# Another order of work and another set of load sizes for a sum of reciprocals

## The chip, the core and the metric

The kernel runs on one core of a Trainium2 chip. Five engines work side by side, each with its own queue of instructions that it runs in order: TensorE (PE in the profile) for matrix products, VectorE (DVE), ScalarE (ACT) and GpSimd (POOL) for elementwise work, and SyncE (SP), which here only issues transfers. Transfers from device memory (HBM) are carried out by 16 DMA engines. The metric is the time of one execution on the device, in microseconds (us); lower is better.

## What is computed

The input holds 32 x 512 = 16384 vectors of 1024 positive numbers in float32, 67.1 MB. The output is the sum of the reciprocals of each vector.

```python
x = np.abs(np.random.randn(32, 512, 1024)).astype(np.float32) + 1e-6

def reference(x):
    return np.sum(1.0 / x, axis=-1).astype(np.float32)
```

## The kernel before

**Tiling.** The 16384 vectors are laid over 128 partitions, 128 vectors on each. A "row" of the kernel is one vector on each partition: 128 partitions x 1024 numbers, 512 KB. There are 128 rows, 0 to 127. The last two, 126 and 127, are cut into halves of 512 columns. The halves have the numbers 126 to 129: first the left halves of both rows, then the right halves. So the list below counts 130 pieces.

**The arithmetic.** A row is halved, into x0 and x1 of 512 columns each, and 1/x0 + 1/x1 is taken as (x0 + x1) / (x0 x1). With S = 2^17 as a scale, ACT computes exp(-ln(S x0 x1)), which is the reciprocal of the product. Two ways lead from there to the sum:

- With an S step, PE adds the halves by two products with the identity matrix into one bank of PSUM (its accumulator memory, 8 banks). DVE then multiplies the 512 reciprocals by the 512 sums and accumulates.
- Without an S step, ACT writes its reciprocals into a PSUM bank, and DVE multiplies all 1024 inputs of the row by them (each reciprocal used twice) and accumulates. This leaves PE out and costs DVE more.

**The buffers.** `ring` holds 40 rows of input, and row q stands at place q % 40. A load of row q therefore waits until row q - 40 has been read for the last time. `prod` holds 22 slots of products, `ps` the 8 PSUM banks, `sums` the 128 results of each partition.

**The order.** Nothing is scheduled by a planner at build time. The order is the list `PLAN`, written out in the source, and the loop at its end issues each token in turn, so the order of the tokens of one engine is the order of that engine's queue. The number after the letter is the row (for D the number of rows), `+n` means n rows in one instruction, `@b` a bank or, for L, a slot:

- `D` (line 185, SP): load the next rows in one transfer. A load also waits, in this build, for the completion of the load eight before it, since eight completion counters are used in turn.
- `P` (line 197, POOL): the product x0 x1 into a slot. `C` with `V` (lines 207 and 218): the same product by PE and DVE, where PE first copies x1 into a bank. `W` (line 218): the same by DVE alone.
- `L` (line 240, ACT): Ln of the slot, with scale S. `E` (line 249, ACT): Exp of its negative, into the slot, or with `@b` into a bank.
- `S` (line 230, PE): the sum of the halves into a bank.
- `R` (line 265, DVE): the multiplication and the accumulation; it frees the bank, the slot and the place in the ring.

`place()` tells where a piece lies in its row. `rows()` names the parts of rows that a step touches, from which `note()` works out which waits are already implied by others. Everything is in one pass; the result is stored by one transfer at the end (line 282).

Two short stretches of the list of before show its style: pairs in the middle, single rows at the end.

```python
L26+2@4 C35@3 E26+2 S27@1 P30+2 V35 L28+2@8 R26 S30@2 R27 E28+2@6
L123@6 R122 L124@7 W125 S125@1 E123@7 E124@6 R123 P126
```

Of the kernel before, what the change touches and what calls it, by code (L numbers as in the profile page):

```python
# [11 lines left out]
def kernel(  # L12
# [9 lines left out]
    H = D // 2  # L22
    F = 128
    R = 40
    NP = 22
    LAST = F - 2  # L26
    S = float(2**17)


# [3 lines left out]

    PLAN = """
        D2 D10 D14 D14 P0+2 C3@3 S2@0 V3 P2 L0+2@0 C11@3 S3@1 E0+2@6 P4+2 V11 L2+2@2 R0 S6@2
        E2+2 R1 P6+2 L4+2@4 R2 R3 E4+2@6 S7@0 P8+2 L6+2@8 R4 S10@1 E6+2 R5 P10 L8+2@10 R6 R7
        S11@2 E8+2@6 L10+2@6 R8 E10+2 R9 D11 R10 R11 P12+2 C19@3 S14@0 V19 P14+2 L12+2@12  # L40
        S15@1 E12+2@6 S18@2 R12 P16+2 L14+2@16 R13 E14+2 R14 P18 L16+2@18 R15 S19@0 E16+2@6
        P20+2 L18+2@14 R16 S22@1 E18+2 R17 D9 P22+2 L20+2@20 R18 R19 E20+2@6 S23@2 P24+2
        L22+2@0 R20 E22+2 R21 L24+2@2 R22 R23 E24+2@6 P26 C27@3 R24 S26@0 P28+2 V27 R25 D7
        L26+2@4 C35@3 E26+2 S27@1 P30+2 V35 L28+2@8 R26 S30@2 R27 E28+2@6 P32+2 L30+2@10 R28
        S31@0 E30+2 R29 P34 L32+2@12 S34@1 R30 R31 E32+2@6 P36+2 S35@0 L34+2@6 R32 E34+2 R33
        D7 P38+2 S38@2 L36+2@16 R34 R35 E36+2@6 S39@1 P40+2 L38+2@18 R36 C43@3 E38+2 R37 D6
        S42@0 P42 L40+2@14 V43 R38 E40+2@6 P44+2 R39 S43@2 L42+2@20 R40 E42+2 S46@1 R41 D3
        P46+2 L44+2@0 R42 R43 E44+2@6 S47@0 P48+2 L46+2@2 R44 S50@2 E46+2 R45 P50 L48+2@4
        R46 C51@3 R47 E48+2@6 S51@1 P52+2 V51 R48 D6 L50+2@8 C59@3 E50+2 R49 P54+2 S54@0
        L52+2@10 V59 R50 E52+2@6 R51 S55@2 P56+2 L54+2@12 R52 E54+2 S58@1 R53 D5 P58  # L50
        L56+2@16 R54 R55 E56+2@6 S59@0 P60+2 L58+2@6 R56 S62@2 E58+2 R57 D4 P62+2 L60+2@14
        R58 R59 E60+2@6 S63@1 P64+2 L62+2@18 R60 S66@0 E62+2 R61 D4 P66 L64+2@20 R62 C67@3
        R63 E64+2@6 P68+2 S67@2 V67 R64 L66+2@0 S70@1 R65 D4 E66+2 P70+2 L68+2@2 R66 R67
        S71@0 E68+2@6 P72+2 L70+2@4 R68 D3 E70+2 R69 D2 C75@3 P74 L72+2@10 S74@2 R70 V75
        P76+2 E72+2@6 R71 S75@1 L74+2@8 R72 D2 E74+2 R73 D2 P80 S78@0 L76+2@12 R74 P81
        L80@16 R75 S79@2 E76+2@6 P78+2 L81@17 R76 D2 S81@1 E80@5 E81 R80 L78+2@6 W82 E78+2
        R81 R77 D1 D1 D1 D1 D1 P88 C85@6 S85@1 R78 P83 L88@18 V85 E88@7 R79 P84 S84@0
        L82+2@14 R88 E82+2@5 P86+2 L84+2@19 R82 D1 E84+2 R83 D1 D1 D1 C90@7 P91 L86+2@0
        S91@2 R85 P93 V90 E86+2@5 R84 P92 S90@1 L90+2@2 R87 L93@21 W89 L92@10 R86 D1 D1 D1
        D1 E93@7 P94 S97@0 E92@6 R93 E90+2 P97 S94@3 L89@11 R92 E89@7 P95 L97@8 R91 S95@4  # L60
        E97 R90 L94+2@4 W96 R97 P101 C99@6 L96@9 R89 E94+2 S100@0 P98 V99 E96@5 L101@12 R95
        P100 S99@1 L98@13 R96 E101@7 L99+2@16 R101 E98@6 P104 C103@5 R94 E99+2 S105@2 R98
        P102 L104@18 V103 E104@7 W105 L102+2@6 R100 P107+2 C106@6 L105@14 R104 E102+2@4
        S108@0 V106 E105 R102 L106+3@19 P109 S107@3 R103 P110 E106+3 R105 S106@4 R99 P111+2
        L109+2@0 R107 S112@1 R108 E109+2@6 R106 L111+2@10 P114 R109 S111@0 E111+2 R110 P113
        L114@15 R111 C115@7 P116 L113@2 R112 E114@6 V115 E113@5 S117@0 P117 R114 L116@3
        L115@8 P118 E116@7 R113 S118@1 E115@6 P119 L117+2@12 R116 E117+2 R115 P120 S120@2
        L119@9 R117 P121 L120@4 S121@3 R118 E119@7 E120 R119 P122 L121@5 S122@0 E121 R120
        P123 L122@18 R121 E122 W124 L123@6 R122 L124@7 W125 S125@1 E123@7 E124@6 R123 P126
        L125@14 P127 L126@16 S127@0 R124 E125 P128 L127@17 S128@2 E126@7 P129 R125 E127  # L70
        S129@3 L128@19 R126 L129@20 E128 R127 E129 R128 R129
    """.split()

    Ln = mybir.ActivationFunctionType.Ln
# [37 lines left out]
    def place(r):  # L112
        if r < LAST:
            return r, 0, H
        part, q = divmod(r - LAST, F - LAST)
        return LAST + q, part * H, H // 2

    def xs(r, h):
        q, at, w = place(r)
        return ring[:, q % R, at + h * w : at + (h + 1) * w]  # L120
# [43 lines left out]
    def rows(r, n, h=None):  # L164
        spaces = []
        for q, at, w in (place(i) for i in range(r, r + n)):
            end = at + 2 * w
            if h is not None:
                at, end = at + h * w, at + (h + 1) * w
            spaces += [("row", q % R, i) for i in range(at, end, H // 2)]  # L170
        return spaces

    def slots(r, n):
# [2 lines left out]
    with tc.manual_schedule():  # L176
        for op, r, n, b in ops:
            p = pslot.get(r)
            if op == "D":
                n, r = r, loaded  # L180
                while n:
                    q, at, w = place(r)
                    a = q % R
                    m = min(n, R - a, LAST - r) if r < LAST else 1
                    inst = nc.sync.dma_start(  # L185
                        out=ring[:, a : a + m, at : at + 2 * w],
                        in_=x_v[:, q : q + m, at : at + 2 * w],
                    )
                    note("SP", inst, writes=rows(r, m))
                    r, n = r + m, n - m  # L190
                loaded = r
            elif op == "P":
                while n:
                    q, at, w = place(r)
                    a, p = q % R, pslot[r]
                    m = min(n, R - a)
                    inst = nc.gpsimd.tensor_tensor(  # L197
                        out=prod[:, p : p + m, :w],
                        in0=ring[:, a : a + m, at : at + w],
                        in1=ring[:, a : a + m, at + w : at + 2 * w],  # L200
                        op=mult,
                    )
                    note("POOL", inst, rows(r, m), slots(r, m))
                    r, n = r + m, n - m
            elif op == "C":
# [6 lines left out]
                    stop=True,  # L212
                )
                note("PE", inst, rows(r, 1, 1), [("bank", b)])
            elif op in "WV":
                w = place(r)[2]
# [38 lines left out]
            elif op == "R":  # L255
                q, at, w = place(r)
                other = ps[:, bank[r], :w]
                if r in halves:
                    row = prod[:, p, :w]
                else:  # L260
                    row = ring[:, q % R, at : at + 2 * w]
                    row = row.rearrange("p (h e) -> p h e", h=2)
# [50 lines left out]
```

## Time and profile before

| | us |
|---|---|
| six runs, median (lowest to highest) | 168.38 (168.25 to 172.23) |
| the profiled execution | 168.25 |
| its span, first to last instruction | 166.4 |
| busy: PE, ACT | 132.5 each |
| busy: DVE, POOL | 128.4, 128.2 |
| share of the DMA engines' time in the loads | 95.1% |

The span is 1.85 us shorter than the time of its own execution. In the profile a row of slices has 40 digits, one for each fortieth of the span (4.16 us), in tenths of full use. "Landing" of a load means that all 16 DMA engines have reported their part. A wait names the last thing that released it. Of PE the list shows each 32-bit product as two matrix instructions, which is why an S step, with two products, makes four, and a C step two.

### The profile page before, as it was taken

Reading aid. Unit: us, or ns where it says so; the run is one execution under the profiler, and the core shown is the slowest. Engines: PE = TensorE matmul, PEld = TensorE weight load, DVE = VectorE, ACT = ScalarE, POOL = GpSimd, SP = SyncE. Lnnn points to the kernel's source line nnn. Section 1 sums busy time; section 2 is a strip of 40 time slices with the busy share of each in tenths; the row PEclk is TensorE's granted clock in tenths of the full one; section 3 lists DMA queues with packets and bytes.
Section 4 is the critical chain, followed back from the end, with each engine's and each line's share of the span. In section 5 each row is a group of like instructions: output and inputs, shape, how many; then the busy total and the mean of one; then the engine's idle time right before and its main releaser. Section 6 shows DMA issues by size and latency. Waiting matters only on the chain.

```text
span 166.4 us, 1340 instructions
## 1 busy us (share of the span) xinstructions
PE 132.5 (80%) x292; PEld 55.5 (33%) x292; DVE 128.4 (77%) x282; ACT 132.5 (80%) x157; POOL 128.2 (77%) x81
## 2 busy tenths in 40 slices
PE   0000799769956999999999999989599979989882
PEld 0000343234312444444433433334234324423351
DVE  0000149855787699799998898989999999999993
ACT  3040067919994899999799999997999998999992
POOL 1500795069995999999999999949977869999860
PEclk9999999969996999999999999999999999999999
DMA  5999999999998989999999999999999999999930
GB/s 195 530 394 394 441 441 441 441 441 441 441 441 381 487 379 424 429 423 438 434 441 441 410 419 458 411 422 430 417 429 433 418 414 425 411 408 410 400 113 18
DMA packets 4904, 67.26 MB, mean 404 GB/s; under 512 B 544, under 2 KB 672, under 8 KB 2336
## 3 DMA queue, kind: packets, MB, share of 16 engines
q1 hardware_dynamic: 4896, 67.18, 95.1%
q8 instruction: 2, 0.03, 0.1%
q14 instruction: 6, 0.05, 0.1%
HBM read 67.11 MB, written 0.07 MB: 404 GB/s over the span
## 4 chain that ended last, share of the span: by engine, by line
DMA 55%; PE 18%; POOL 9%; ACT 8%; DVE 6%; issue 2%; SPq 1%; POOLq 0%; DVEq 0%
DMA ring<-in_x_dram 55%; PE ps L230 15%; POOL prod L197 9%; ACT prod L240 4%; DVE ring L265 3%; PE ps L207 3%; ACT ps L249 3%; DVE prod L265 2%; ACT prod L249 2%; DVE prod L218 1%; SPq L185 1%; DVE sums L265 0%; POOLq L197 0%; DVEq L308 0%
## 5 line engine op out<-in xcount | busy, mean ns | idle before, releaser
L197 POOL TENSOR_TENSOR prod<-ring 128x1024 f32<-128x1024 f32 (+2 forms) x75 | 127.5, 1736 | 33.3 <-DMA ring<-in_x_dram 27.6
L230 PE MATMUL ps<-ring,ident 128*128 128x512 f32 (+1 forms) x260 | 116.4, 595 | 3.9 <-DVE sums L265 3.4
L240 ACT ACTIVATE prod<-prod 128x1024 f32<-128x1024 f32 (+2 forms) x78 | 68.6, 892 | 25.9 <-DVE prod L218 14.2
L265 DVE CUSTOM_DVE_ANT_1 ring<-ring,ps 128x1024 f32<-128x1024 f32 (+1 forms) x65 | 76.4, 1209 | 7.7 <-ACT ps L249 7.5
L230 PEld LDWEIGHTS ps<-ring,ident 128*128 128x128 f32 x260 | 49.5, 195 | 70.9 <-issue 53.0
L265 DVE CUSTOM_DVE_ANT_0 prod<-prod,ps 128x512 f32<-128x512 f32 (+1 forms) x63 | 41.0, 679 | 0.6 <-PE ps L230 0.4
L207 PE MATMUL ps<-ring,ident 128*128 128x512 f32 x32 | 19.9, 709 | 26.8 <-DMA ring<-in_x_dram 26.4
L249 ACT ACTIVATE ps<-prod 128x1024 f32<-128x1024 f32 (+2 forms) x41 | 34.1, 838 | 3.3 <-DVE sums L265 2.5
L249 ACT ACTIVATE prod<-prod 128x1024 f32<-128x1024 f32 (+3 forms) x37 | 34.4, 932 | 0.9
L218 DVE TENSOR_TENSOR prod<-ring,ps 128x512 f32<-128x512 f32 x16 | 11.0, 685 | 27.2 <-PE ps L207 27.2
L207 PEld LDWEIGHTS ps<-ring,ident 128*128 128x128 f32 x32 | 5.9, 212 | 36.4 <-issue 20.8
L265 DVE DVE_READ_ACCUMULATOR2_ANT sums<- 128x1 f32 x130 | 10.7, 83 | 0.0
L218 DVE TENSOR_TENSOR prod<-ring 128x512 f32<-128x512 f32 x6 | 4.1, 688 | 0.1
L83 ACT ACT_TABLE_LOAD x1 | 1.3, 1283 | 0.7 <-PEq L297 0.7
L265 DVE CUSTOM_DVE_ANT_0 prod<-prod,ps,sums 128x256 f32<-128x256 f32 x2 | 0.9, 476 | 0.0
masks.py:197 POOL MEMSET ident<- 128x128 f32 x1 | 0.2, 205 | 0.3 <-POOLq L297 0.3
masks.py:199 POOL TENSOR_SCALAR_AFFINE_SELECT ident<-ident 128x128 f32<-128x128 f32 x1 | 0.3, 294 | 0.1
L297 POOL MEMSET const-float32-0.0<- 128x1 f32 x1 | 0.1, 99 | 0.2 <-issue 0.2
L297 POOL MEMSET const-bfloat16-1.0<- 128x1 bf16 x1 | 0.1, 102 | 0.0
L297 POOL MEMSET const-uint8-127<- 128x1 uint8 x1 | 0.1, 102 | 0.0
L297 POOL MEMSET const-float32-1.0<- 128x1 f32 x1 | 0.1, 99 | 0.0
## 6 DMA issues: line engine op xcount, KB each, us to landing
ring<-in_x_dram SPq DMA_DIRECT2D x2, 7168.0 KB, 41.2
ring<-in_x_dram SPq DMA_DIRECT2D x2, 3584.0 KB, 29.2
ring<-in_x_dram SPq DMA_DIRECT2D x2, 3072.0 KB, 31.7
ring<-in_x_dram SPq DMA_DIRECT2D x3, 2048.0 KB, 33.7
ring<-in_x_dram SPq DMA_DIRECT2D x1, 5632.0 KB, 31.7
ring<-in_x_dram SPq DMA_DIRECT2D x5, 1024.0 KB, 32.0
ring<-in_x_dram SPq DMA_DIRECT2D x1, 5120.0 KB, 16.5
ring<-in_x_dram SPq DMA_DIRECT2D x1, 4608.0 KB, 30.8
```

What stands on the lines that cost most here:

```text
L83: nc.scalar.add_instruction(mybir.InstLoadActFuncSet(name=nc.get_next_instruction_name(), act_func_set_id=act_sets.index("natural_log_exp_ ...
L185: inst = nc.sync.dma_start(out=ring[:, a : a + m, at : at + 2 * w], in_=x_v[:, q : q + m, at : at + 2 * w],)
L197: inst = nc.gpsimd.tensor_tensor(out=prod[:, p : p + m, :w], in0=ring[:, a : a + m, at : at + w], in1=ring[:, a : a + m, at + w : at + 2 * w],
L207: inst = nc.tensor.matmul(ps[:, b, : place(r)[2]], lhsT=ident, rhs=xs(r, 1), start=True, stop=True,)
L218: inst = nc.vector.tensor_tensor(out=prod[:, p, :w], in0=xs(r, 0), in1=in1, op=mult)
L230: inst = nc.tensor.matmul(ps[:, b, : place(r)[2]], lhsT=ident, rhs=xs(r, h), start=h == 0, stop=h == 1,)
L240: inst = nc.scalar.activation(out=pg, in_=pg, func=Ln, scale=S)
L249: inst = nc.scalar.activation(out=rc, in_=pg, func=Exp, scale=-1.0)
L265: inst = nc.vector.tensor_tensor_reduce(out=row, in0=row, in1=other, scale=S, scalar=total if q in summed else 0.0, op0=mult, op1=add, acc ...
L297: nc = _bacc.Bacc("TRN2", target_bir_lowering=False, num_devices=1)
```

## The change

The list is replaced by another that loads 2, 10, 16, 12, 12, 10, 9, 3, 6, 7, 6, 5, 4, 2, 3, 3 rows, then five times 2, then six single rows and the four half rows: 31 loads in place of 33. The first 40 rows, which fill the ring, come as 2, 10, 16 and 12 rows instead of 2, 10, 14 and 14. The steps of rows 12 to 79 keep their kind with a few moves (row 27 gets its product by C and V earlier in the list, some slots and banks are others). From row 80 on rows are taken in another order, other rows get S steps, and other rows are grouped. In all, one row more has an S step (66 instead of 65, of 130), V and W stay at 16 and 6, ACT has one triple more and two pairs fewer of Ln (48) as well as of Exp (48), and six rather than nine single rows are loaded at the end.

The half rows are now written as a table, `PARTS`, with the same four halves in the same order, and `rows()` names parts of 128 columns instead of 256.

```diff
-    LAST = F - 2
+    PARTS = [(126, 0, 512), (127, 0, 512), (126, 512, 512), (127, 512, 512)]
+    LAST = PARTS[0][0]
     S = float(2**17)
     PLAN = """
-        D2 D10 D14 D14 P0+2 C3@3 S2@0 V3 P2 L0+2@0 C11@3 S3@1 E0+2@6 P4+2 V11 L2+2@2 R0 S6@2
+        D2 D10 D16 D12 P0+2 C3@3 S2@0 V3 P2 L0+2@0 C11@3 S3@1 E0+2@6 P4+2 V11 L2+2@2 R0 S6@2
...
-        S11@2 E8+2@6 L10+2@6 R8 E10+2 R9 D11 R10 R11 P12+2 C19@3 S14@0 V19 P14+2 L12+2@12
-        S15@1 E12+2@6 S18@2 R12 P16+2 L14+2@16 R13 E14+2 R14 P18 L16+2@18 R15 S19@0 E16+2@6
+        S11@2 E8+2@6 L10+2@6 R8 E10+2 R9 D12 R10 R11 P12+2 C19@3 S14@0 V19 P14+2 L12+2@12
+        C27@3 S15@1 E12+2@6 V27 R12 P16+2 L14+2@16 S18@2 R13 E14+2 R14 P18 L16+2@20 R15
...
-        P76+2 E72+2@6 R71 S75@1 L74+2@8 R72 D2 E74+2 R73 D2 P80 S78@0 L76+2@12 R74 P81
-        L80@16 R75 S79@2 E76+2@6 P78+2 L81@17 R76 D2 S81@1 E80@5 E81 R80 L78+2@6 W82 E78+2
-        R81 R77 D1 D1 D1 D1 D1 P88 C85@6 S85@1 R78 P83 L88@18 V85 E88@7 R79 P84 S84@0
+        P76+2 R71 S75@1 L74+2@4 R72 E74+2 S78@2 R73 D2 D2 P78+2 L76+2@12 R74 R75 E76+2@6
+        S79@0 L78+2@16 R76 P80 C83@5 E78+2 R77 D2 D2 P81 S84@1 L80@20 V83 E80@7 P84 R78
+        L81@21 S83@3 R80 D1 L83@10 P85 E81@6 R79 E83 S82@2 W82 L84@11 W86 E84 L82@2 R83
+        L85+2@14 R81 D1 D1 D1 D1 P90+2 S87@0 E82 R84 E85+2@6 R82 C92@5 R85 D1 P87+3 L90+2@0
+        S88@1 V92 E90+2@3 R86 D1 D1 D1 D1 S89@2 L92@3 R91 E92@6 L87+3@6 P97 C96@7 R90 S96@4
...
+        L94+2@4 R96 S101@0 V98 E93@6 P99 E94+2@4 R93 S103@1 P101+2 L99+2@12 R94 L98@20 R95
+        E99+2@6 S102@2 P103 E98@4 R100 S104@3 P105 L101+3@14 R98 P106 R99 E101+3 P104
...
+        S113@0 R108 P112 L113@6 E110+2 R109 P115 S115@3 E113 R110 L112@7 P114 L115@8 R113
+        E112@7 R111 S117@0 E115 P116 R112 L114@18 E114@6 W117 L116@19 R114 L117@9 P118
+        C119@7 E116@5 R115 S119@1 E117 V119 P120 L118@4 R117 L119@5 R116 E118@7 P121 S121@2
+        E119 R118 L120@12 P122 L121@13 S122@0 E120@6 R119 E121 W123 L122@20 R120 S123@1
+        L123@14 P124 E122 R121 E123 W125 S124@3 L124@15 R122 P126 L125@16 R123 E124 P127
+        S126@0 E125@7 R124 P128 L127@11 S128@1 R125 L126@10 P129 E127@6 E126 S129@2 L129@1
+        R127 L128@0 R126 E129 E128 R129 R128
     """.split()
...
-        part, q = divmod(r - LAST, F - LAST)
-        return LAST + q, part * H, H // 2
+        q, at, length = PARTS[r - LAST]
+        return q, at, length // 2
...
-            spaces += [("row", q % R, i) for i in range(at, end, H // 2)]
+            spaces += [("row", q % R, i) for i in range(at, end, H // 4)]
```

More of the change, by code (lines that the diff above doesn't have):

```diff
@@ L25 @@
     NP = 22
-    LAST = F - 2
+    PARTS = [(126, 0, 512), (127, 0, 512), (126, 512, 512), (127, 512, 512)]
+    LAST = PARTS[0][0]
     S = float(2**17)
     PLAN = """
-        D2 D10 D14 D14 P0+2 C3@3 S2@0 V3 P2 L0+2@0 C11@3 S3@1 E0+2@6 P4+2 V11 L2+2@2 R0 S6@2
+        D2 D10 D16 D12 P0+2 C3@3 S2@0 V3 P2 L0+2@0 C11@3 S3@1 E0+2@6 P4+2 V11 L2+2@2 R0 S6@2
         E2+2 R1 P6+2 L4+2@4 R2 R3 E4+2@6 S7@0 P8+2 L6+2@8 R4 S10@1 E6+2 R5 P10 L8+2@10 R6 R7
-        S11@2 E8+2@6 L10+2@6 R8 E10+2 R9 D11 R10 R11 P12+2 C19@3 S14@0 V19 P14+2 L12+2@12
-        S15@1 E12+2@6 S18@2 R12 P16+2 L14+2@16 R13 E14+2 R14 P18 L16+2@18 R15 S19@0 E16+2@6
[L42 to L54, printed above, removed]
-        P76+2 E72+2@6 R71 S75@1 L74+2@8 R72 D2 E74+2 R73 D2 P80 S78@0 L76+2@12 R74 P81
-        L80@16 R75 S79@2 E76+2@6 P78+2 L81@17 R76 D2 S81@1 E80@5 E81 R80 L78+2@6 W82 E78+2
-        R81 R77 D1 D1 D1 D1 D1 P88 C85@6 S85@1 R78 P83 L88@18 V85 E88@7 R79 P84 S84@0
[L58 to L71, printed above, removed]
@@ new lines @@
+        S11@2 E8+2@6 L10+2@6 R8 E10+2 R9 D12 R10 R11 P12+2 C19@3 S14@0 V19 P14+2 L12+2@12
+        C27@3 S15@1 E12+2@6 V27 R12 P16+2 L14+2@16 S18@2 R13 E14+2 R14 P18 L16+2@20 R15
+        S19@0 E16+2@6 P20+2 L18+2@14 R16 S22@1 E18+2 R17 P22+2 L20+2@0 R18 R19 E20+2@6 S23@2
+        P24+2 L22+2@2 R20 S26@0 E22+2 R21 D10 P26 L24+2@4 R22 C35@3 R23 E24+2@6 S27@1 P28+2
+        V35 L26+2@18 R24 S30@2 E26+2 R25 P30+2 L28+2@8 R26 R27 E28+2@6 S31@0 P32+2 L30+2@6
+        R28 S34@1 E30+2 R29 D9 P34 L32+2@12 R30 R31 S35@2 E32+2@6 P36+2 L34+2@10 R32 S38@0
@@ new lines @@
+        E34+2 R33 D3 P38+2 L36+2@16 R34 R35 E36+2@6 S39@1 L38+2@20 R36 P40+2 C43@3 E38+2 R37
+        D6 S42@2 V43 P42 L40+2@14 R38 C51@3 R39 E40+2@6 P44+2 S43@0 V51 L42+2@0 R40 S46@1
+        E42+2 R41 P46+2 L44+2@2 R42 R43 E44+2@6 S47@2 P48+2 L46+2@18 R44 S50@0 E46+2 R45 D7
+        P50 L48+2@8 R46 R47 S51@1 E48+2@6 P52+2 L50+2@4 R48 C59@3 E50+2 R49 S54@2 P54+2
+        L52+2@6 V59 R50 E52+2@6 R51 S55@0 P56+2 L54+2@12 R52 D6 E54+2 R53 S58@1 P58 L56+2@16
+        R54 R55 S59@2 E56+2@6 P60+2 L58+2@10 R56 E58+2 R57 D5 P62+2 C67@3 L60+2@20 R58 S62@0
@@ new lines @@
+        V67 E60+2@6 R59 P64+2 L62+2@14 R60 S63@1 E62+2 R61 D4 D2 S66@2 P66 L64+2@2 R62 R63
+        E64+2@6 P68+2 S67@0 L66+2@0 R64 S70@1 E66+2 R65 D3 P70+2 L68+2@18 R66 R67 E68+2@6
+        S71@2 P72+2 L70+2@8 R68 C75@3 E70+2 R69 D3 D2 S74@0 P74 L72+2@6 V75 R70 E72+2@6
+        P76+2 R71 S75@1 L74+2@4 R72 E74+2 S78@2 R73 D2 D2 P78+2 L76+2@12 R74 R75 E76+2@6
+        S79@0 L78+2@16 R76 P80 C83@5 E78+2 R77 D2 D2 P81 S84@1 L80@20 V83 E80@7 P84 R78
+        L81@21 S83@3 R80 D1 L83@10 P85 E81@6 R79 E83 S82@2 W82 L84@11 W86 E84 L82@2 R83
@@ new lines @@
+        L85+2@14 R81 D1 D1 D1 D1 P90+2 S87@0 E82 R84 E85+2@6 R82 C92@5 R85 D1 P87+3 L90+2@0
+        S88@1 V92 E90+2@3 R86 D1 D1 D1 D1 S89@2 L92@3 R91 E92@6 L87+3@6 P97 C96@7 R90 S96@4
+        V96 P95 E87+3 R92 P93 S97@3 L96+2@18 R89 R88 E96+2 P94 R87 L93@9 R97 C98@7 P100
+        L94+2@4 R96 S101@0 V98 E93@6 P99 E94+2@4 R93 S103@1 P101+2 L99+2@12 R94 L98@20 R95
+        E99+2@6 S102@2 P103 E98@4 R100 S104@3 P105 L101+3@14 R98 P106 R99 E101+3 P104
+        L105+2@10 R102 C109@7 R101 P107 L104@21 R103 E105+2@5 S107@0 V109 P108 E104 R105
@@ new lines @@
+        L107@17 S110@1 P111 L108+2@0 R106 E107 W110 S111@2 E108+2@6 R107 P113 L110+2@2 R104
+        S113@0 R108 P112 L113@6 E110+2 R109 P115 S115@3 E113 R110 L112@7 P114 L115@8 R113
[3 more added lines that the diff above has]
+        L123@14 P124 E122 R121 E123 W125 S124@3 L124@15 R122 P126 L125@16 R123 E124 P127
```

## The prediction

> **What bounds the kernel now.** I read the page's busy times and slices first, then its DMA queues.
>
> ```profile
> PE 132.5 (80%) x292; PEld 55.5 (33%) x292; DVE 128.4 (77%) x282; ACT 132.5 (80%) x157; POOL 128.2 (77%) x81
> DVE  0000149855787699799998898989999999999993
> ACT  3040067919994899999799999997999998999992
> DMA  5999999999998989999999999999999999999930
> GB/s 195 530 394 394 441 441 441 441 441 441 441 441 381 487 379 424 429 423 438 434 441 441 410 419 458 411 422 430 417 429 433 418 414 425 411 408 410 400 113 18
> q1 hardware_dynamic: 4896, 67.18, 95.1%
> q8 instruction: 2, 0.03, 0.1%
> q14 instruction: 6, 0.05, 0.1%
> ```
>
> Four engines have 128 to 132 us of work each and one stream of loads fills 95.1% of the DMA time. The loads never stop; the engines stop only early. Next, the chain of waits in order of time (start, length, what):
>
> ```profile
> 2.10 49.41 DMA ring<-in_x_dram
> 81.11 31.30 DMA ring<-in_x_dram
> 147.07 10.17 DMA ring<-in_x_dram
> 158.69 1.72 PE ps L230 x4
> 163.51 0.40 DVE prod L265
> ```
>
> It goes through three loads: the one that lands at 51.51, at 112.40 (81.11+31.30) and at 157.24. The last 6.7 us are a relay of engines. Then busy time by stretch of the trace, cut at landings (columns: length, then PE, PEld, DVE, ACT, POOL busy, clock, DMA share, GB/s):
>
> ```profile
> 34.00:51.50 17.50, 13.33 (x26) 5.33 (x26) 12.25 (x29) 13.88 (x14) 15.21 (x7) 0.90 0.97 421
> 51.50:66.00 14.50, 14.45 (x30) 6.46 (x31) 11.70 (x25) 11.79 (x13) 14.36 (x8) 0.88 0.99 427
> 66.00:85.50 19.50, 19.50 (x46) 8.37 (x45) 17.73 (x40) 18.22 (x19) 19.50 (x10) 1.00 0.98 420
> 85.50:112.40 26.90, 25.15 (x56) 9.84 (x54) 24.40 (x54) 26.26 (x29) 24.02 (x13) 1.00 1.01 430
> 112.40:147.00 34.60, 31.23 (x70) 12.88 (x70) 34.23 (x74) 32.81 (x42) 29.50 (x21) 1.00 1.00 421
> 147.00:161.10 14.10, 12.59 (x29) 5.36 (x30) 13.98 (x32) 13.91 (x26) 12.08 (x12) 1.00 0.90 353
> ```
>
> From 112.4 on DVE works 34.23 of 34.60 us and then 13.98 of 14.10: no slack. ACT has little. So data and engines finish together. Last, the end, in the timeline:
>
> ```profile
> 158.69 4.54 PE L230 MATMUL ps<-ring,ident 128*128 128x512 f32 x16 [1.11 <-DVE sums L265]
> 159.32 2.81 POOL L197 TENSOR_TENSOR prod<-ring 128x256 f32<-128x256 f32 x4 [1.92 <-DVE prod L218]
> 161.88 0.71 ACT L240 ACTIVATE prod<-prod 128x256 f32<-128x256 f32 x2
> 163.43 0.48 DVE L265 CUSTOM_DVE_ANT_0 prod<-prod,ps,sums 128x256 f32<-128x256 f32 x1
> 163.94 0.34 SPq L282 DMA_DIRECT2D out_dram<-sums  x1
> ```
>
> The last half row lands at 161.10, POOL ends at 162.12, PE at 163.24, ACT at 163.20, DVE at 163.92; the store follows. PE still has a wait of 1.11 us there.
>
> **What the Trainium skill says.** "DMA: Bandwidth & Descriptors", Rules for kernel authors, wants loads of at least 1 MiB for full bandwidth. The trace agrees mildly: a 512 KB row alone takes 1.28 us, two rows 2.48, seven 8.51. "Runtime: NRT & Kernel Launch", Instruction fetch mechanics, says that each engine's instructions are refilled by DMA in 16 KiB blocks, the cost "mostly hidden". Here it is not free: the q8 and q14 packets come in the middle of the loads, and after them the sixteen completion marks of a load spread out. The load of 9 rows has fourteen of them by 75.75 us, then 76.27 and 77.06. A load is complete with its slowest DMA engine. "TensorE: Matmul & The Clock Gate", Part 1, describes a half clock set over windows of 3413 ns after idling. The trace agrees: half clock at 34.41 to 37.82 and at 51.48 to 54.89, each after PE had waited for a load. "Perfetto Trace Analysis", Optimizing Scalar/DVE Operations, says grouping pays since every operation has its own overhead. Here an ACT pair takes 0.96 us from start to next start and a single 0.52, so 1.02 against 1.04 us a row for Ln and Exp: hardly a difference, save where an Exp directly follows the Ln of its own row (0.65 single, 1.07 pair).
>
> **The change part by part.** All durations, spacings and landings are read from the trace of the one profiled execution. The list differs from its first load on, not only from row 80.
>
> *PARTS and the finer steps in rows().* They name the same four half rows in the same order. Nothing.
>
> *Loads.* Loads fit 1.209 us a row plus 0.065 us a load (7 rows 8.53, single 1.27). There are 31 instead of 33: 0.13 us less, so the last half row lands at 160.97 and, counting back, rows 118 and 119 at 150.7, row 125 at 158.4. Rows 12 to 27 come as one load and land at 17.63+16x1.21=37.0 instead of 34.57 (rows 12 to 25); rows 28 to 39 land at 51.5 as before.
> Can the queue run dry? A load waits for the rows that it overwrites and for the landing of the load eight before it. Before, rows 40 to 50 were issued at 33.6 and begun at 51.5. The twelve rows after the change wait for R11, which ended at 34.7 and comes from data landed at 17.6, so at about 35. Ten more rows wait for R21: about 50, wanted at 66. Margins are over 15 us; later they grow (issued 98.9, landed 133.4 before). No cost; without this cover each us late would be a us.
>
> *Start of the second load.* POOL's pair takes 2.34, so ACT starts row 12 at 37.0+2.4=39.4 instead of 37.0: 2.4 late. But before, ACT then idled 2.45 us (52.0 to 54.45) for the load at 51.51. Now it has 16 rows: 16x1.02=16.3, with its gaps about 56.2, when POOL has just finished rows 28 and 29 (55.9). The idling disappears and the lateness with it: 28 rows are done at 56.2, before at 56.6. PE too keeps its clock at 51.5.
>
> *Middle.* Rows 40 on land at 66.6 (straggling DMA engine counted as before, 0.55), plus POOL 2.4: ACT reaches row 40 at 69.05, before 68.79. Row 52: landing 79.5, ACT 81.95 (82.09 before). Row 62: landing 90.4, ACT 92.85 (92.27). Row 76: about 107 (106.91).
>
> *From row 76 on, by engine.* Counts by start-to-start spacing (full R 1.14, half-sum R 0.61, V and W 0.60; S 1.72, C 0.93):
> DVE: before 26x1.14+24x0.61+12x0.60+0.6+3x0.4=53.3, after 25 and 25, so 52.8.
> ACT: 53.8 before, 53.3 after (four adjacent single Ln-Exp instead of six, four adjacent pairs instead of seven, one more triple).
> PE from S78: 24x1.72+6x0.93+2.6=49.4 before, 25x1.72+... = 51.1 after: 1.7 more.
> POOL: 49.1 and 48.9.
> So DVE and ACT gain half a us, PE loses 1.7 us of its 8 us of idling.
>
> *The end, carried forward by hand* with these spacings and the landings above, each step at the latest of its data, its engine, its bank. ACT waits 0.9 for POOL's pair of rows 90 and 91 (landed 117.3, ready 119.7), with E90+2, L92 and L87+3 queued behind it and R91, R90 on DVE waiting for those; 0.25 at L87+3, 0.45 at L101+3; and it stands at 143.55 with 110 rows done, where before it had 110 done between 142.6 and 144.6. From there everything comes back to back: E125 ends near 160.6, the last Exp near 163.2 (before 163.20). DVE: W125 must wait for row 125 at 158.4; then 0.60+3x0.61+1.14+0.61+2x0.37+0.48=5.4 gives 163.8. PE: C119 starts at 150.7, then 0.93+5x1.72 for S119, S121 to S124 (160.2), 2x0.86+1.03 for the half rows: S129 ends at 163.0 with no idle left; then R129 and R128 add 0.37+0.5, so 163.9. S124 also delays R124 to 160.4, which makes DVE end near 164.0.
>
> **Sum.** The last R ends at 163.9 to 164.1 against 163.92. Out-store and end 2.5, as now: span 166.4 to 166.6. The profiled execution took 168.25 with span 166.4, so 1.85 lie outside; it was 0.13 under the median 168.38. That gives 168.4 to 168.6; I take **168.5**.
>
> **The rivals.**
> *PE becomes the last engine (slower).* Place: C119 to S129, 12.3 us without a gap. It decides once C119 starts later than about 150.9. What can hold it is bank 7, which R112 frees, by my count at 149.35. Only 1.4 us of cover; R112 hangs on ACT's E112 and the whole row order since 104. For it: PE has 1.7 us more to do, and in the page's slices it is at 9 nearly throughout. Against: its banks come free early in my count. If R112 slips by 2.3, the end moves by 0.9: 169.4.
> *A straggling DMA engine (slower).* Two 16 KB instruction packets (taking 1.02 and 1.09 us) and several of 8 KB hit different engines of the sixteen, and the last load's marks spread over 1.9 us (159.20 to 161.10). If another list moves two of them to the same engine, the stream ends 0.8 to 1.3 later: 169.4. Against: six runs of the kernel before nearly agree, so the placement is not random.
> *The same, favourably (faster).* If the slowest engine misses one, the stream ends 0.5 to 0.8 earlier and engines with half a us in hand follow: 167.8.
> *The late start is not absorbed (slower).* If ACT cannot work through from 39.4 to 56.2, say because POOL or PE at half clock (to about 41) hold it, most of 2.4 us stays: 169.9. Against: in 34 to 51.5 ACT did 14 rows in 15 us, idling only 0.4.
>
> **How the numbers follow.** Five of the six runs before lie within 168.25 to 168.46, so 0.2% (0.34 us) is about what can be told from no change. Chances: forecast, within 168.04 to 168.72, 0.40; PE or row order slips, 169.4, 0.30; straggler, 169.4, 0.12; late start, 169.9, 0.08; faster, 167.8, 0.10. So faster 0.10, same 0.40, slower 0.50: no single slower mechanism beats the forecast, together they do. The range 167.9 to 169.8 leaves out the outer parts of the fast and late cases. The forecast's own range is 168.1 to 168.7.
>
> **What would show it.** Right: rows 12 to 27 landing near 37.0; no ACT idling at 52 to 54; full clock from about 41 on; last load at 161.0; PE without a gap from 150.7; last DVE near 164. Wrong: C119 waiting for DVE past 151; ACT idling over 1 us in one place after 117; last landing off 161.0 by over 0.5; SP's loads reaching an empty queue.

## The result and the profile after

The changed kernel took 168.78 us in the median, the kernel before 168.46 in the same comparison: a ratio of 1.0022 with a 95% interval of 1.0013 to 1.0031. Measured once more (the last experiment below) it took 168.62 against 168.44, a ratio of 1.0008, interval 0.9998 to 1.0018. So the change costs something between nothing and 0.3%, about a quarter of a microsecond. The prediction took 0.2% (0.34 us) as what can be told from no change: the first measurement sits on that bound, the second is under it. The forecast was 168.5.

The first profile of the changed kernel is a late one: its own execution took 169.18 with a span of 167.4. Its page shows the same picture as before, lines of busy time, slices and DMA queues:

```profile
PE 134.0 (80%) x296; PEld 55.8 (33%) x296; DVE 127.6 (76%) x282; ACT 132.5 (79%) x157; POOL 127.9 (76%) x80
ACT  3040073934899999899989999999799989999991
q1 hardware_dynamic: 4608, 67.18, 94.8%
```

PE has 1.5 us more work (the one S step more), DVE 0.8 less. The loads fill nearly the same share of the DMA time. Why this execution was late, the landings tell: the second load landed at 18.24 us instead of 17.63; of its packets, four at 11 us took 2.0 to 2.2 us instead of 1.5. The whole stream stayed 0.5 to 0.6 us late, to a last landing at 161.57. The first two loads are the same in both kernels, and in the twelve other profiles of this study the second one landed between 17.44 and 17.68, so this is an accident of one execution and not of the change. The profile of the second measurement (execution 168.60, span 166.8) has its last landing at 161.05, and is used from here on where an end is read.

Busy time by stretch, first profile of the changed kernel (length, then PE, PEld, DVE, ACT, POOL busy, clock, DMA share, GB/s):

```profile
34.00:51.50 17.50, 13.63 (x28) 5.80 (x29) 11.30 (x27) 11.68 (x12) 13.84 (x7) 0.90 1.00 427
51.50:66.00 14.50, 13.91 (x32) 5.45 (x30) 13.61 (x30) 14.28 (x15) 14.50 (x8) 1.00 0.98 425
...
112.40:147.00 34.60, 31.50 (x73) 13.12 (x72) 33.72 (x73) 32.78 (x42) 30.51 (x22) 1.00 1.00 422
147.00:161.10 14.10, 13.31 (x32) 5.50 (x31) 13.96 (x34) 13.97 (x27) 10.89 (x10) 1.00 0.91 359
```

In the first stretch ACT works 11.68 us, before 13.88: the larger load lets it start later. In the second it works 14.28 of 14.50, before 11.79, and PE keeps its full clock (1.00, before 0.88): most of the lateness is won back there. In the last, PE is busy 13.31 of 14.10 us, before 12.59.

The chain of waits of the second profile, its end (start, length, what):

```profile
128.53 22.22 DMA ring<-in_x_dram
150.75 0.14 issue
150.89 1.10 PE ps L207 x2
151.99 8.60 PE ps L230 x20
...
160.72 0.11 DVE prod L265
```

Before, the chain's last load was row 124, at 157.24, and the rest was a relay. Now it is the pair of rows 118 and 119, landing at 150.75, and from there one engine carries it: C119 and five S steps of PE, to R124. The timeline says the same, second profile, PE and then DVE:

```profile
150.89 1.10 PE L207 MATMUL ps<-ring,ident 128*128 128x512 f32 x2 [0.54 <-DMA ring<-in_x_dram]
151.82 11.34 PE L230 MATMUL ps<-ring,ident 128*128 128x512 f32 x32
160.72 0.69 DVE L265 CUSTOM_DVE_ANT_0 prod<-prod,ps 128x512 f32<-128x512 f32 x1 [0.32 <-PE ps L230]
163.90 0.48 DVE L265 CUSTOM_DVE_ANT_0 prod<-prod,ps,sums 128x256 f32<-128x256 f32 x1
```

32 matrix instructions in 11.34 us without a gap, and one wait of DVE, 0.32 us, for the S step of row 124. The kernel before had a gap of 1.11 us in that place.

### The profile page after: what moved, and what is told of

Its sections match the earlier page's. It is cut to its first block, busy times and chain, and to the rows that moved or that the text cites. A ratio compares the mean times of both kernels' runs of the same rounds, so it can differ in the third digit from the quotient of the medians.

```text
span 167.4 us, 1330 instructions
## 1 busy us (share of the span) xinstructions
PE 134.0 (80%) x296; PEld 55.8 (33%) x296; DVE 127.6 (76%) x282; ACT 132.5 (79%) x157; POOL 127.9 (76%) x80
## 3 DMA queue, kind: packets, MB, share of 16 engines
q1 hardware_dynamic: 4608, 67.18, 94.8%
## 4 chain that ended last, share of the span: by engine, by line
DMA 70%; PE 9%; DVE 6%; POOL 6%; issue 5%; ACT 2%; SPq 0%; DVEq 0%; POOLq 0%
DMA ring<-in_x_dram 70%; PE ps L230 6%; POOL prod L197 6%; DVE ring L265 4%; PE ps L207 2%; DVE prod L265 2%; ACT ps L249 1%; ACT prod L240 1%; DVE sums L265 0%; SPq L185 0%; DVE prod L218 0%; DVEq L265 0%; POOLq L197 0%; DVEq L308 0%
## 5 line engine op out<-in xcount | busy, mean ns | idle before, releaser
L230 PE MATMUL ps<-ring,ident 128*128 128x512 f32 (+1 forms) x264 | 119.5, 598 | 3.8 <-DVE sums L265 2.4
L240 ACT ACTIVATE prod<-prod 128x1024 f32<-128x1024 f32 (+3 forms) x78 | 68.3, 892 | 25.7 <-POOL prod L197 14.2
L265 DVE CUSTOM_DVE_ANT_1 ring<-ring,ps 128x1024 f32<-128x1024 f32 x64 | 75.1, 1209 | 6.2 <-ACT ps L249 6.1
L265 DVE CUSTOM_DVE_ANT_0 prod<-prod,ps 128x512 f32<-128x512 f32 x64 | 41.3, 678 | 0.8 <-ACT prod L249 0.4
L207 PE MATMUL ps<-ring,ident 128*128 128x512 f32 x32 | 18.8, 673 | 26.0 <-DMA ring<-in_x_dram 25.6
L249 ACT ACTIVATE ps<-prod 128x1024 f32<-128x1024 f32 (+2 forms) x38 | 33.4, 881 | 4.3 <-DVE sums L265 3.6
L249 ACT ACTIVATE prod<-prod 128x1024 f32<-128x1024 f32 (+3 forms) x40 | 35.1, 885 | 0.8
```

The source lines that it names most:

```text
L207: inst = nc.tensor.matmul(ps[:, b, : place(r)[2]], lhsT=ident, rhs=xs(r, 1), start=True, stop=True,)
L230: inst = nc.tensor.matmul(ps[:, b, : place(r)[2]], lhsT=ident, rhs=xs(r, h), start=h == 0, stop=h == 1,)
L240: inst = nc.scalar.activation(out=pg, in_=pg, func=Ln, scale=S)
L249: inst = nc.scalar.activation(out=rc, in_=pg, func=Exp, scale=-1.0)
L265: inst = nc.vector.tensor_tensor_reduce(out=row, in0=row, in1=other, scale=S, scalar=total if q in summed else 0.0, op0=mult, op1=add, acc ...
```

## The experiments

Four theories were on trial. Theory 1: the end of the changed list costs the time, first of all PE's run from C119 to S129. Theory 2: the loads cost it. Theory 3: the later start of the compute at 37 us costs it. Theory 4, added after the first runs: every wait of DVE in the last 50 us adds to the end.

One figure of each trace decides more than the times do: how long after the last landing DVE ends. The second column tells whose order the rows from 72 on have.

| kernel | last rows as | loads | last landing | DVE ends | later by |
|---|---|---|---|---|---|
| before | before | 33 | 161.10 | 163.92 | 2.81 |
| changed, first profile | changed | 31 | 161.57 | 164.98 | 3.41 |
| changed, second (e11) | changed | 31 | 161.05 | 164.39 | 3.34 |
| e1 | changed | 31 | 161.08 | 164.39 | 3.30 |
| e5 | before | 33 | 161.29 | 164.13 | 2.84 |
| e4, no C119 | changed | 31 | 160.93 | 164.30 | 3.37 |
| e6, more PE work | changed | 31 | 160.97 | 165.23 | 4.26 |
| e7, more PE work | before | 33 | 161.30 | 164.12 | 2.83 |
| e8, four edits | changed | 31 | 161.16 | 165.30 | 4.14 |
| e9, no S124 | changed | 31 | 160.99 | 164.06 | 3.07 |
| e10, no triple | changed | 31 | 160.98 | 164.36 | 3.38 |

**Half and half (e1, e2, e5).** e1 takes everything of rows below 72 and the loads of the first 80 rows from the kernel before, the rest from the changed one; e2 and e5 the other way round.

```diff
# e1: the rows below 72 and the first loads of before, then the changed list
-D2 D10 D16 D12 ... D12 ... D10 ... D9 ... D3 ... D6
+D2 D10 D14 D14 ... D11 ... D9 ... D7 ... D7 ... D6
 ... P72+2 ... S74@0 P74 L72+2@6 V75 ... R129 R128
```

> Rows below 72 and the loads of the first 80 rows as before, rows from 72 on and the loads from row 80 on as after the change. Theory 1 (TensorE's gapless run from C119 to S129 at the end costs the time): about 168.8, with C119 to S129 again without a gap and the last DVE step 3.3 to 3.4 us after the last landing. Theory 2 (the loads of the first 80 rows cost it) and theory 3 (the later start of the compute at 37.6 instead of 34.6 costs it): about 168.4, and 2.8 us after the last landing.

Measured: 168.64 against 168.36, ratio 1.0021 (1.0012 to 1.0029). That is the changed kernel's time, with the old first loads. In this kernel the sums of rows 70 and 71 are not what they should be: a slot, and for row 71 a bank too, is taken by rows 74 and 75 before their last read. R70 waits 0.34 us for that, which is made up by the end: W125 begins at 158.56, right after row 125 has landed (158.52). PE's run is there (C119 at 150.97, S129 ending at 163.24, no gap), and DVE ends 3.30 us after the last landing. Theories 2 (first loads) and 3 fall by this.

> The other half: rows below 72 and the loads of the first 80 rows as after the change, the rest as before. Theory 1: about 168.4, with the last DVE step about 2.8 us after the last landing. Theory 2 in the first loads, and theory 3: about 168.8.

e2 gave 172.57, ratio 1.0243, which none of the theories had. Here too places of rows 70 and 71 were taken early, and it mattered more, as the waits from 95 to 125 us show (who waited for whom: total, times, longest):

```profile
ACT prod L240 <- DVE sums L265: 1.5, 1, 1.5
DVE prod L265 <- POOL prod L197: 1.1, 1, 1.1
```

The Ln of rows 74 and 75 waits for R70 and R71, and R70 for the product of row 74. These waits are only a part of the 4.2 us: later four W steps of DVE take 1.15 to 1.61 us instead of 0.69, 2.75 us more in all, since each meets a product of POOL (see the last section). The run says nothing of the change. e5 repeats it with two names changed, so that every value lives long enough:

```diff
-L70+2@8 ... S71@2
+L70+2@4 ... S71@0
```

> The hybrid again with a slot and a bank renamed so that nothing is reused early: rows below 72 and the loads of the first 80 rows as after the change, rows from 72 on and the loads from row 80 on as before. Theory 1 (the tail of the changed list costs the time, first of all TensorE's gapless run at the end): 168.3 to 168.5, last DVE step about 2.8 us after the last landing. Theory 2 (first loads) and theory 3 (late start): 168.8.

Measured: 168.41 against 168.35, ratio 1.0005 (0.9996 to 1.0014), 2.84 us after the last landing, with the compute started as late as in the changed kernel. The timeline of PE in e5 has the gap of the kernel before again:

```profile
149.55 8.24 PE L230 MATMUL ps<-ring,ident 128*128 128x512 f32 x18
158.87 4.54 PE L230 MATMUL ps<-ring,ident 128*128 128x512 f32 x16 [1.07 <-DVE sums L265]
```

So what the change costs comes with the rows from 72 on or with the loads from row 80 on, which e1 and e5 exchange together. No run separates the two. Against the loads speaks that row 119, for which C119 waits, lands at 150.84 as a single row before and at 150.75 in its pair after.

**The changed order with the loads of before (e3).** Only the D tokens are exchanged, so that the four engines keep the changed order.

> The changed order of all four compute engines with the 33 loads of before. Theory 1: 168.8 or 0.1 more, since rows 118 and 119 land at nearly the same time as single rows. Theory 2 (load sizes): back to 168.4. Theory 3: back to 168.4 too, since rows 12 to 25 land at 34.6 again.

Measured: 180.04, ratio 1.0691. All three expectations missed. The changed list has C27 and V27 ahead of S15 and R12, since it counts on row 27 in the load that lands at 37. With the old loads row 27 lands at 51.5, and two queues stand still behind it. Timeline of e3, PE and then DVE:

```profile
51.67 2.04 PE L207 MATMUL ps<-ring,ident 128*128 128x512 f32 x2 [14.20 <-DMA ring<-in_x_dram]
53.75 0.69 DVE L218 TENSOR_TENSOR prod<-ring,ps 128x512 f32<-128x512 f32 x1 [17.15 <-PE ps L207]
```

The experiment cannot separate loads from order; it shows that the two halves of such a list belong together. I should have seen it in the list.

**Less work for PE (e4).**

```diff
-C119@7 ... V119
+W119
```

> The changed kernel with the product of row 119 made by DVE alone (W119) in place of C119 on PE and V119 on DVE. DVE does the same, PE 0.93 us less just before its gapless run. Theory 1: S129 ends up to 0.9 earlier against the last landing, the last DVE step 0.25 to 0.5 earlier: 168.3 to 168.5. Theories 2 and 3: 168.8 as the changed kernel.

Measured: 168.60, ratio 1.0013 (1.0004 to 1.0022). This misses the 168.3 to 168.5 of theory 1 and cannot be told from the two measurements of the changed kernel. The trace says why so little: without C119 PE reaches S121 early, and then waits for row 121 to land. PE in e4:

```profile
150.71 1.99 PE L230 MATMUL ps<-ring,ident 128*128 128x512 f32 x4 [0.44 <-DMA ring<-in_x_dram]
153.37 9.70 PE L230 MATMUL ps<-ring,ident 128*128 128x512 f32 x28 [0.68 <-DVE sums L265]
```

The wait of 0.68 is put down to DVE, but the bank had been free since 148.4; row 121 landed at 153.23, so it was the load. S121 thus starts 0.68 us later than the end of S119 would have allowed, only 0.17 us ahead of where C119 had put it (153.54 in the second profile), and R124 still waits 0.25 us. Four S steps in a row from one landing suffice: 4 x 1.72 us of PE for rows that land every 1.28 us.

**More work for PE (e6, e7).** A copy of half a row to a bank that nobody reads, after S122, in the changed kernel and in the kernel before.

```diff
 S122@0
+C122@5
```

> The changed kernel with one useless copy of half a row by PE (0.93 us) between S122 and S123; nothing reads it. Theory 1: S124 ends 0.93 later and R124 and all that follows with it: 169.6 to 169.7. Theory 4 (DVE's own work and its earlier waits set the end, PE is only just in time): up to 0.3 of it is seen, 168.8 to 169.1.

> The kernel before with the same useless copy at the same place, after S122. PE idles 1.12 us there before S125, so under every theory that leaves the kernel before bound by DVE and the data the copy is hidden: 168.3 to 168.5. If PE bound the end there too: 169.3.

Measured: e6 169.45, ratio 1.0066 (1.0050 to 1.0081); e7 168.36, ratio 0.9997 (0.9989 to 1.0005). Against the second profile, DVE ends 0.84 us later in e6 (165.23 against 164.39), nearly all of the 0.86 us between the start of the copy and that of S123, and 0.92 us later after the last landing. This is the wait in front of R124 in e6, in DVE's timeline, and the place of the copy in e7, in PE's:

```profile
161.55 0.69 DVE L265 CUSTOM_DVE_ANT_0 prod<-prod,ps 128x512 f32<-128x512 f32 x1 [1.03 <-ACT prod L240]
```

```profile
157.62 1.02 PE L207 MATMUL ps<-ring,ident 128*128 128x512 f32 x2
158.87 4.54 PE L230 MATMUL ps<-ring,ident 128*128 128x512 f32 x16 [0.23 <-DVE sums L265]
```

In e6 the wait before R124 grew from 0.32 to 1.03 us (it is named after ACT, whose E124 had ended before; the last product of S124 ended at 161.41). In e7 the copy filled the gap, 1.11 us in the kernel before, to 0.23 and cost nothing. So PE binds at the end of the changed kernel, and not in the kernel before.

**Without S124 (e9).** Row 124's sum of halves is left out; everything else stays.

```diff
-                for h in range(2):
+                for h in range(2 * (r != 124)):
```

> The changed kernel without the four matrix instructions of S124; R124 multiplies by what the bank holds from row 115, so the sum of row 124 is left out. Nothing else differs, DVE, ACT and POOL do the same steps. Theory 1 in part: R124 loses its wait of 0.25 to 0.34 us, the rest stays: 168.4 to 168.55, last DVE step about 3.1 us after the last landing, because DVE still has one more row pending than the kernel before when row 125 lands. Theory 1 alone (PE makes the whole difference): 168.3, 2.8 us after the last landing. Theory 4 without PE: 168.8.

Measured: 168.31 against 168.44, ratio 0.9988 (0.9978 to 0.9999), on the same chip and in the same comparison as the second measurement of the changed kernel, 168.62. The four matrix instructions are worth 0.31 us. PE's gap is back, and R124 starts at 160.39 where it started at 160.72; e9, PE, ACT (E124) and DVE (R124):

```profile
159.83 2.86 PE L230 MATMUL ps<-ring,ident 128*128 128x256 f32 x12 [0.98 <-DVE sums L265]
159.75 0.61 ACT L249 ACTIVATE prod<-prod 128x512 f32<-128x512 f32 x1
160.39 0.69 DVE L265 CUSTOM_DVE_ANT_0 prod<-prod,ps 128x512 f32<-128x512 f32 x1
```

DVE ends 3.07 us after the last landing. The extra 0.53 us of the changed kernel (3.34 against 2.81) is thus halved: 0.27 of it is the wait for S124, and 0.26 remains. The next in line is ACT: R124 now starts 0.03 us after E124 has ended (160.36), and R129 0.04 after E129 (163.13).

**Without a triple (e10).** DVE's wait of 0.37 us before R102, for the product of row 103, is taken away.

```diff
-L101+3@14 ... E101+3 ... L105+2@10
+L101+2@14 ... E101+2 L103@16 ... L105+2@10 E103
```

> The changed kernel with the Ln and Exp triple of rows 101 to 103 as a pair and a single, so that R102 no longer waits 0.37 us for P103. If each wait of DVE adds to the end (theory 4): 0.3 to 0.4 less, 168.4 to 168.5. If later landings and S124 set the end anew (theory 1): 168.7 to 168.9, DVE then waits more at W125 or R124.

Measured: 168.60, ratio 1.0013 (1.0003 to 1.0023): no gain. All the waits of DVE from 136 us on in e10:

```profile
138.85 0.69 DVE L265 CUSTOM_DVE_ANT_0 prod<-prod,ps 128x512 f32<-128x512 f32 x1 [0.23 <-ACT prod L249]
160.68 0.69 DVE L265 CUSTOM_DVE_ANT_0 prod<-prod,ps 128x512 f32<-128x512 f32 x1 [0.34 <-PE ps L230]
```

The wait before R102 became one of 0.23 before R103, and R124 starts when it did. Only 0.14 us of waiting was thus taken away, too little for the times to decide. The trace tells where it went: in the second profile DVE reaches W125 at 158.49, just after row 125 has landed (158.47), and in e10 at 158.45 (158.41), so that hardly anything saved ahead of W125 can reach the end. That, and the 0.84 us of e6 where theory 4 allowed 0.3, is against theory 4.

**Four edits at once (e8).** W119; the triple split; P123 on POOL for W123 on DVE; row 124 without S.

```diff
-C119@7 ... V119 ... L101+3@14 ... W123 ... S124@3 ... E124
+W119 ... L101+2@14 ... L103@16 ... P123 ... E124@3
```

> The changed kernel with four edits of its tail: W119 for C119 and V119; the triple of rows 101 to 103 as a pair and a single, so that R102 need not wait for P103; P123 on POOL, which idles there, instead of W123 on DVE; row 124 without an S step (its Exp goes to bank 3), which takes 1.72 us off PE and adds 0.53 to DVE. By the trace of the changed kernel: no wait for S124 (-0.3), R102 0.37 earlier, +0.53, -0.60: the last DVE step about 0.7 earlier, then held by the last landing and the half rows. Theories 1 and 4: 168.1 to 168.4. Theories 2 and 3: 168.8.

Measured: 169.42, ratio 1.0060 (1.0047 to 1.0073), as slow as e6. DVE in e8:

```profile
158.64 0.87 DVE L218 TENSOR_TENSOR prod<-ring 128x512 f32<-128x512 f32 x1 [0.36 <-DMA ring<-in_x_dram]
160.99 1.22 DVE L265 CUSTOM_DVE_ANT_1 ring<-ring,ps 128x1024 f32<-128x1024 f32 x1 [0.26 <-ACT ps L249]
```

The 0.60 us taken off DVE (W123) ended in a wait of 0.36 for row 125 to land at 158.62, before W125. The 0.53 us put on DVE (R124 now takes a full row, 1.22) came after it, where nothing hides it. And POOL fell behind: its product of row 120 met W119 and took 1.69 us instead of 1.28 (see the last section), and P123 came on top. ACT therefore waited 0.18 us before L121 and 0.27 before L123, so that R124 waits again, now for its Exp; and W125 took 0.87 instead of 0.69 while POOL was still at row 124. My sum added the four savings as if one place were as good as another.

**The changed kernel again (e11).**

> The changed kernel once more, for a second profile. The landing of the second load, 0.6 us late in the first profile (18.24), should be near 17.5 as in the other runs, the last landing near 161.0, and the last DVE step 3.3 to 3.4 us after it under theory 1; 168.7 to 168.8 without the profile.

Measured: 168.62, ratio 1.0008 (0.9998 to 1.0018). In this list some D tokens stand elsewhere among those of the other engines; the order of every queue and the loads are those of the changed kernel. The second load landed at 17.65, the last at 161.05, DVE ended 3.34 us after it, as theory 1 had it.

No version tried here beats the kernel before; e9 leaves work out.

## Why the prediction was right, and where it was off

The time, 168.78 and then 168.62, lies near the forecast of 168.5 and in the range of 167.9 to 169.8; the forecast's own range, 168.1 to 168.7, holds the second and not the first. Against the kernel before it is 0.32 and 0.18 us more, where 0.12 was forecast. The shape of the forecast holds: a few tenths gained in the loads and lost at the end. Part of the closeness is luck. The span was forecast at 166.4 to 166.6 and came out at 166.8 in the second profile, while what was added for the time outside the span and for a profile faster than the median, 1.85 + 0.13 us, came out at 1.80 + 0.02: the second error hides half of the first. By its steps:

- *Loads, 0.13 us saved, last landing 160.97.* Right. Seven profiles with 31 loads, the disturbed first one aside, land between 160.93 and 161.16, at 161.02 in the mean. The kernel before, e5 and e7, with 33 loads, land at 161.10, 161.29 and 161.30, so the saving is rather 0.2 us, and in the profile that the prediction read they landed early. This 0.2 taken from the 0.53 us lost at the end leaves 0.3, and the times show 0.2 to 0.3. The queue never ran dry; the smallest margin before row 80 was 13.1 us (rows 52 to 61), not over 15.
- *The later start is absorbed.* Right, but later than forecast. The load of 16 rows landed at 37.6, in the second profile at 37.0; ACT's idling of 2.45 us at 52 is gone, the clock stays up. ACT has 28 rows done at 57.3 instead of 56.2 (56.6 before) and reaches row 76 at 107.8 instead of about 107. By the end nothing is left of it: e1 and e5 show that the head of the list makes no difference to the time.
- *The middle, and ACT's three waits of 0.9, 0.25 and 0.45 us.* Measured in the second profile 0.71, 0.13 and 0.43.
- *PE has no idling left after C119, and S124 delays R124.* Right in kind; e6, e7 and e9 show it. It was under-sized: R124 was put at 160.4 and came at 160.72 in the second profile. Of these 0.32 us, 0.05 is a later landing (150.75) and 0.14 lies between it and the start of C119; most of the rest is the end of S124, which takes 1.88 us, while I had added 1.72, the distance of two starts.
- *The last DVE step at 163.9 to 164.1.* Measured 164.39: R124 came 0.32 us late, and R128 another 0.08, for which the profile names no wait. Of the lag of 0.53 us against the kernel before, the 0.26 that e9 keeps has several small parts, read from the traces and not tried. In e9 DVE needs 5.58 us from W125 to the end, in the kernel before 5.34. Of the 0.24 between them, 0.08 is work: behind W125 stand four rows, R122 to R125, three of them half-sum rows (2.97 us by the spacings of the prediction), before it was three, two of them full (2.89). The rest is mostly ACT: R124 starts 0.08 later than DVE could, after E124, and R129 0.07 later, after E129. The prediction had the last Exp near 163.2, as before; it ends at 163.45 in the second profile.

The rival "PE becomes the last engine" had the right engine and place and the wrong trigger: C119 did not wait for bank 7 and R112, it waited for its own row (R112 ended at 149.63, row 119 landed at 150.75). The straggling DMA engine did not come, neither for better nor for worse: the marks of the last load spread over 2.28 us in the first profile (159.29 to 161.57) and over 1.79 us in the second, against 1.9 before, and the profiles with 31 loads end where the fit said. The late start is refuted by e1 and e5.

## What to carry to other kernels

Where a stream of data sets the pace and the engines keep up with little to spare, the cost of an order is decided after the last loads: count for each engine the work that can only start once a given late load has landed, and compare 1.72 us of one engine for each row with the 1.28 us at which rows land. Time saved ahead of such a landing is handed back in the wait for it (e8, e10), time added behind it is paid in full (e6), and idle time of an engine that is last in nothing is free (e7). An edit that moves a product to an engine can also lengthen a step of another one beside it (e8). A list of loads and a list of work that rely on each other cannot be exchanged one by one (e3).

## What the runs showed of the hardware beyond that

- In one execution of thirteen, four packets of the second load took 2.0 to 2.2 us instead of 1.5 at 11 us, and the stream of loads stayed 0.5 to 0.6 us late to its end. The DMA engines have hardly any idle time (94.8% in the loads), so nothing made up for it.
- A W step of DVE, whose two inputs both lie in `ring`, and a product of POOL held each other up. A W step begun while a product was running ended 0.55 us after that product, though it never took less than 0.69: this holds within 0.01 us for all 79 W steps of the thirteen profiles. A product begun within a W step, more than 0.14 us before its end, was late in turn: nine single rows took 1.67 to 1.75 us instead of 1.28 (three in e2, three in e3, one each in e4, e5 and e8). As an example, W96 in e2 began 1.06 us before the second of these two products ended; e2, POOL and DVE:

```profile
130.24 2.50 POOL L197 TENSOR_TENSOR prod<-ring 128x512 f32<-128x512 f32 x2
131.68 1.61 DVE L218 TENSOR_TENSOR prod<-ring 128x512 f32<-128x512 f32 x1
```

V steps, which read one input from PSUM, took at most 0.69 us, though a product of POOL ran beside 202 of the 208 for 0.3 us or more; nor were the R steps of full rows lengthened (1.22 us at most). In the kernel before and in the changed one no W step begins with more than 0.14 us of a product left, so neither pays for it. All this is read from the traces; no run was made to try it.
